# Splitting one more store of a DMA-bound rotary-score kernel over its DMA engines

## The chip, the cores and the metric

The kernel runs on one core of one Trainium2 chip. The metric is device time in microseconds (us), lower is better. A core has 16 DMA engines; "landing" means the semaphore update by which one of them reports that its part of a transfer has arrived.

## The reference

```python
batch, seq, heads, dim = 16, 512, 16, 64        # all float32
q_rot = concat([q1*cos - q2*sin, q1*sin + q2*cos])   # k_rot likewise
scores = einsum('bshd,bthd->bsht', q_rot, k_rot)     # (16, 512, 16, 512)
```

Inputs are 2 x 33.5 MB, the output is 268 MB. Writing it is most of the work.

## The kernel before

There are 64 steps, four per batch. A step makes 128 rows of one batch's output for all 16 heads in a staging tile of 128 x 8192 floats (4096 KB), copied there from PSUM by ACT, and stores it (the four steps of the first batch store theirs in parts of 1024 KB). There are three staging buffers.

```python
stage_pool = ctx.enter_context(tc.tile_pool(name="stage", bufs=3))
...
    def store(i, st):
        o = o_v[i // C, i % C]
        if i < NST - 1:                              # NST = 64, the number of steps
            nc.sync.dma_start(o, st)                 # 128 rows of 32 KB
            return

        h = H - 2
        nc.sync.dma_start(o[:, :h], st[:, :h])       # 14 heads, 128 rows of 28 KB
        nc.sync.dma_start(o[:116, h:], st[:116, h:]) # 2 heads, 116 rows of 4 KB
        nc.sync.dma_start(o[116:, h:], st[116:, h:]) # 2 heads, 12 rows
...
        nc.scalar.copy(out=so, in_=si)               # L173: PSUM to staging, 8 per step
```

128 rows are shared by 16 engines, 8 rows each. 116 = 4 x 29 rows go to the first four engines, 12 rows to twelve; the trace shows 16, 4 and 12 landings, and the prediction below says why. So a split store takes bytes off the other engines and gives them to the first four.

## Time and profile before

| | before |
|---|---|
| time, the first three runs | 800.7 us (800.0 to 800.71) |
| bytes moved, mean rate | 336.17 MB, 421 GB/s |
| DMA queue 1 busy | 98.6% of 16 engines' span |
| PE, ACT, DVE busy | 87%, 70%, 68% |

When a queue is busy 98.6% of the span on average, the average no longer tells much. What counts is the engine that ends last. The profile's views sum over the engines; the landings, read one by one from the trace, show the single engine. The prediction below shows both.

### The profile page before, as it was taken

How to read it: one execution, taken by the hardware profiler on the slowest of the kernel's cores; microseconds unless marked ns; L12 is line 12 of the kernel's file. 1: busy time of each engine (PE TensorE's matmuls, PEld its weight loads, DVE VectorE, ACT ScalarE, POOL GpSimd, SP SyncE). 2: the span in 40 equal slices, each digit the busy share in tenths (PEclk: the TensorE clock that was granted, in tenths of full speed). 3: DMA queues.
4: the chain of work that ended last, by engine and by line, in shares of the span. 5: the costliest groups of instructions: out<-in, count | busy, mean ns of one | idle time of the engine just before them, and what ended most of it. 6: DMA issues, size and time to landing. Idle time of an engine off the chain costs nothing.

```text
span 799.0 us, 7715 instructions
## 1 busy us (share of the span) xinstructions
PE 691.3 (87%) x3072; PEld 299.3 (37%) x3072; DVE 544.6 (68%) x516; ACT 561.2 (70%) x647; POOL 0.7 (0%) x6
## 2 busy tenths in 40 slices
PE   4989998997979979799797997979979799799970
PEld 2444443343434334343343443424434343344420
DVE  6999987676866768577585775857758478585300
ACT  3888886775857758577585775757757677578870
POOL 0000000000000000000000000000000000000000
PEclk9999999898998989889898898988989899899995
DMA  9999999999999999999999999999999999998995
GB/s 355 422 424 424 432 427 433 425 435 427 421 437 426 439 427 430 433 431 430 431 428 433 434 428 429 433 438 420 418 426 434 435 415 418 426 440 375 422 439 231
DMA packets 17844, 336.17 MB, mean 421 GB/s; under 512 B 1808, under 2 KB 3088, under 8 KB 4240
## 3 DMA queue, kind: packets, MB, share of 16 engines
q1 hardware_dynamic: 17520, 335.55, 98.6%
q8 instruction: 24, 0.39, 0.2%
q10 hardware_dynamic: 288, 0.13, 0.1%
q14 instruction: 12, 0.10, 0.0%
HBM read 67.24 MB, written 268.44 MB: 420 GB/s over the span
## 4 chain that ended last, share of the span: by engine, by line
DMA 50%; PE 40%; ACT 4%; DVE 3%; issue 1%; ACTq 0%; SPq 0%; DVEq 0%
DMA out_dram<-st 47%; PE ps L166 30%; PE bank L127 10%; ACT st L173 4%; DMA q_sb<-in_q_dram 2%; DVE part L106 1%; DMA early<-in_k_dram 1%; DVE q_sb L107 0%; DVE k_sb L107 0%; DVE k_sb L111 0%; DVE q_sb L111 0%; DVE early L107 0%; DVE kT_t L142 0%; ACTq L281 0%; DVE early L111 0%
## 5 line engine op out<-in xcount | busy, mean ns | idle before, releaser
L173 ACT COPY st<-ps 128x1024 f32<-128x1024 f32 x512 | 494.7, 1018 | 203.7 <-DMA out_dram<-st 105.6
L166 PE MATMUL ps<-kT_t,qT_t 64*128 64x512 f32 x2048 | 548.9, 654 | 71.0 <-ACT st L173 70.9
L166 PEld LDWEIGHTS ps<-kT_t,qT_t 64*128 64x128 f32 x2048 | 185.0, 197 | 261.7 <-issue 144.6
L142 DVE COPY qT_t<-bank 128x512 f32<-128x512 f32 x118 | 81.6, 691 | 203.8 <-PE bank L127 203.8
L127 PEld LDWEIGHTS bank<-ident,q_sb 128*128 128x128 f32 x480 | 55.6, 152 | 102.5 <-issue 99.1
L127 PE MATMUL bank<-ident,q_sb 128*128 128x128 f32 x480 | 86.9, 308 | 0.9 <-PE ps L166 0.9
L127 PEld LDWEIGHTS bank<-ident,k_sb 128*128 128x128 f32 x480 | 50.5, 141 | 95.4 <-issue 38.7
L127 PE MATMUL bank<-ident,k_sb 128*128 128x128 f32 x480 | 78.7, 287 | 1.6 <-DVE qT_t L142 1.2
L142 ACT COPY kT_t<-bank 128x512 f32<-128x512 f32 x122 | 72.5, 599 | 6.4 <-PE bank L127 6.4
L107 DVE TENSOR_TENSOR q_sb<-q_sb,cos_t 128x1024 f32<-128x1024 f32 x60 | 73.5, 1226 | 2.1
L111 DVE TENSOR_TENSOR k_sb<-k_sb,part 128x1024 f32<-128x1024 f32 x60 | 73.5, 1225 | 2.1
L107 DVE TENSOR_TENSOR k_sb<-k_sb,cos_t 128x1024 f32<-128x1024 f32 x60 | 73.5, 1225 | 2.0
L106 DVE TENSOR_TENSOR part<-q_sb,ss_t 128x1024 f32<-128x1024 f32 x60 | 73.5, 1225 | 2.0
L106 DVE TENSOR_TENSOR part<-k_sb,ss_t 128x1024 f32<-128x1024 f32 x60 | 73.0, 1216 | 0.1
L111 DVE TENSOR_TENSOR q_sb<-q_sb,part 128x1024 f32<-128x1024 f32 x60 | 73.0, 1216 | 0.0
L127 PE MATMUL bank<-ident,early 128*128 128x128 f32 x64 | 10.5, 316 | 12.5 <-DVE early L111 10.6
L127 PEld LDWEIGHTS bank<-ident,early 128*128 128x128 f32 x64 | 8.3, 161 | 17.5 <-issue 13.4
L106 DVE TENSOR_TENSOR part<-early,ss_t 128x1024 f32<-128x1024 f32 x8 | 9.8, 1223 | 5.9 <-DMA early<-in_k_dram 5.8
L111 DVE TENSOR_TENSOR early<-early,part 128x512 f32<-128x512 f32 x16 | 10.3, 687 | 0.2
L107 DVE TENSOR_TENSOR early<-early,cos_t 128x1024 f32<-128x1024 f32 x8 | 9.8, 1225 | 0.3
L142 ACT COPY qT_t<-bank 128x512 f32<-128x512 f32 x10 | 5.7, 617 | 3.2 <-PE bank L127 3.2
L142 DVE COPY kT_t<-bank 128x512 f32<-128x512 f32 x6 | 4.1, 685 | 0.3 <-PE bank L127 0.3
(9 smaller groups left out, 2.8 us busy)
## 6 DMA issues: line engine op xcount, KB each, us to landing
out_dram<-st SPq DMA_DIRECT2D x59, 4096.0 KB, 23.9
k_sb<-in_k_dram SPq DMA_DIRECT2D x15, 2048.0 KB, 26.9
q_sb<-in_q_dram SPq DMA_DIRECT2D x15, 2048.0 KB, 29.9
out_dram<-st SPq DMA_DIRECT2D x16, 1024.0 KB, 14.3
out_dram<-st SPq DMA_DIRECT2D x1, 3584.0 KB, 20.4
early<-in_k_dram SPq DMA_DIRECT2D x1, 1536.0 KB, 8.9
early<-in_q_dram SPq DMA_DIRECT2D x1, 1536.0 KB, 12.1
early<-in_k_dram SPq DMA_DIRECT2D x1, 512.0 KB
```

Of the source, the lines that this page charges most:

```text
L106: nc.vector.tensor_tensor(pv, xs, ss, op=mult)
L107: nc.vector.tensor_tensor(xc, xc, cs, op=mult)
L111: nc.vector.tensor_tensor(y, y, z, op=add)
L127: nc.tensor.transpose(bank[:, x, :], src, ident)
L142: copy(out=dst, in_=src)
L166: nc.tensor.matmul(out=po, lhsT=lhs[64 * r : 64 * r + 64, :], rhs=rh, start=True, stop=True)
L173: nc.scalar.copy(out=so, in_=si)
```

## The change

The intent is to take the split that the last store has and use it a second time, at step 56, so that the engine that ends last has less to write.

```diff
-        if i < NST - 1:
+        if i not in (NST - 8, NST - 1):
             nc.sync.dma_start(o, st)
             return
```

One transfer becomes three.

## The prediction

> **What bounds the kernel now.** I read the page from its DMA part first, because 336 MB pass in 799 us. These are the lines for queues and issues.
>
> ```profile
> DMA packets 17844, 336.17 MB, mean 421 GB/s; under 512 B 1808, under 2 KB 3088, under 8 KB 4240
> ...
> q1 hardware_dynamic: 17520, 335.55, 98.6%
> q8 instruction: 24, 0.39, 0.2%
> ...
> out_dram<-st SPq DMA_DIRECT2D x59, 4096.0 KB, 23.9
> ...
> out_dram<-st SPq DMA_DIRECT2D x1, 3584.0 KB, 20.4
> ...
> out_dram<-st SPq DMA_DIRECT2D x1, 464.0 KB
> ...
> out_dram<-st SPq DMA_DIRECT2D x1, 48.0 KB
> ```
>
> Queue 1 alone keeps the 16 DMA engines busy 98.6% of the span. PE is busy 87%, ACT 70%, DVE 68%. So the transfers bound the kernel, and the question is which of the 16 engines ends last. Next the busy time by stretches at the end (start:end, length, busy us of PE, PEld, DVE, ACT, POOL, granted clock, DMA share, GB/s).
>
> ```profile
> 700.00:727.00 27.00, 24.68 (x112) 10.43 (x108) 20.34 (x20) 19.65 (x24) 0.00 (x0) 0.94 1.00 431
> 727.00:731.00 4.00, 4.00 (x22) 1.72 (x19) 3.22 (x3) 3.77 (x6) 0.00 (x0) 1.00 0.35 147
> 731.00:789.00 58.00, 42.91 (x192) 18.01 (x190) 13.64 (x15) 38.12 (x42) 0.00 (x0) 0.91 1.00 426
> 789.00:795.00 6.00, 0.00 (x0) 0.00 (x0) 0.00 (x0) 0.00 (x0) 0.00 (x0) 0.50 0.30 107
> 795.00:799.00 4.00, 0.00 (x0) 0.00 (x0) 0.00 (x0) 0.00 (x0) 0.00 (x0) 0.50 0.04 15
> ```
>
> Two holes: from 727 to 731 the engines are two thirds idle, and after 789 only a few work; a share of 0.04 is less than one engine of 16 (0.0625). The views do not name an engine, so I read the trace's packet and semaphore records one by one. Every store ends in 16 landings, one per engine. In us, by step, with the time of issue:
>
> ```
> step issued  earliest ... latest but one   last
> 55   695.98  708.02       712.80           719.46
> 56   706.00  717.70       722.48           729.33
> 57   716.02  727.38       732.18           739.30
> 58   730.22  741.14       743.23           749.88
> 60   748.85  760.92       762.57           769.72
> 62   767.60  780.38       782.41           789.24
> 63   777.43  788.89       790.87           797.80  (14 heads)
> 63   778.35  794.22 to 794.95 (4 landings: 116 rows, 2 heads)
> 63   779.10  12 landings, 11 by 795.13, the last 797.99
> ```
>
> **One engine, the straggler, is always last**, 9 to 12 us behind the fastest. Its packets follow each other without a gap from 731 to 797.6 (back-to-back records). It takes about 9.9 us per full store, the others 9.68. The end is its end.
>
> The chain of waits says the same: it goes through store 60 into ACT's first copy of step 63 (start, length, what).
>
> ```profile
> 748.85 20.87 DMA out_dram<-st
> ...
> 769.82 1.02 ACT st L173
> ...
> 777.40 0.92 ACTq L281
> ```
>
> The staging pool has three buffers, so step 63 starts only when all 16 engines have delivered store 60, which is the straggler's 769.72. Steps 62 and 58 do likewise (ACT's timeline):
>
> ```profile
> 719.56 3.84 ACT L173 COPY st<-ps 128x1024 f32<-128x1024 f32 x4 [3.56 <-DMA out_dram<-st]
> ...
> 759.92 7.65 ACT L173 COPY st<-ps 128x1024 f32<-128x1024 f32 x8 [2.30 <-DMA out_dram<-st]
> ```
>
> The line at 719.56 makes the hole: step 58 waits for store 55's last landing (719.46), its store is issued only at 730.22, and by then fast engines have been out of work since 727.4.
>
> **What the Trainium skill says.** "DMA: Bandwidth & Descriptors", section "Why a DMA increments its semaphore by 16 and not by 1": the number of engines is the largest k up to 16 that divides the slowest dimension, on the lowest-numbered engines. So 116 rows go to 4 engines (29 rows each), 12 rows to 12, 128 to 16. The trace agrees: 4 and 12 landings above. The straggler is among the 12, since 797.99 belongs to the 12-row transfer, and not among the first four, which land by 794.95. Same page, "Specifications": about 27 GiB/s an engine; the trace has 32,768 B in 1.213 us, 27.0 GB/s, so the engine is at its rate. Same page, "Latency and other measured facts": engines 7 and 15 are usually slower, put down there to the descriptor rings of GpSimd's path. The trace has one slow engine although GpSimd issues nothing, so the reason given does not fit; the records do not number engines, so whether it is 7 is open.
>
> **The change, part by part.** It takes one 4096 KB store away and puts 3584 KB, 464 KB and 48 KB in its place. Bytes and all compute are the same.
>
> On the straggler: 8 packets of 32,768 B (8 x 1.213 = 9.70 us) become 8 of 28,672 B (1.062 us each in the last store, 8.50) plus one of 4,096 B (0.159) and two more semaphore packets (0.009 each): 8.67. It saves **1.03 us**. It has no gap afterwards, so this should reach the end whole: its last packet at 796.6 instead of 797.63.
>
> On engines 0 to 3: 8 x 1.062, then 29 and 1 packets of 4,096 B. In the last store these 30 took about 5.3 to 6.1 us (the shortest, 0.159 each, would make 4.8). Sum 13.3 to 14.6 against 9.70: **3.6 to 4.9 us more** on each. The hole pays for it if they are among the engines that wait in it. Following packets back to back through the trace, I find 7 engines at 727.4 to 728.0 after step 57, 8 at 728.7 to 732.2, and the straggler. The 8 are those that take turns at the instruction packets of queue 8 (24 packets, three each, some 0.9 us each). Two of those 8 that fetch at 736.6 and 766.1 are single-row engines (4 to 11) in the last store; one engine of the first four fetches from queue 14 at 754.8, and no queue-8 fetch is seen on it. The best reading, not a proof, is that engines 0 to 3 are all in the fast seven. Their last packets of step 57 end at 727.0 to 727.6 (a landing is recorded some 0.36 us after its packet), so they now end at 730.6 to 732.5, while step 58's packets start at 731.05 to 731.20 anyway: a slip of 0 to 1.5 us, with 0.3 us more room at 741. Their last landing goes from 794.95 to between 794.9 and 796.2, still ahead of the straggler's 796.8.
>
> Other parts: two more issues on SP (0.70 and 1.19 us in the last store). SP idles about 10 us between stores and step 57's store comes at 716.02, so they are hidden. Step 59 on ACT now waits for three semaphores instead of one, an estimate of 0.1 us; but store 56 should be complete by 728.3, before step 59 starts at 731. Steps 61 to 63 start up to 1 us earlier, which matters only to the already queued work.
>
> Sum: -1.03 us on the path that sets the end. 800.7 - 1.0 = **799.7 us**, that is 0.13%.
>
> **The rivals.** (1) Engines 0 to 3 take over as the bound. If one is among the lagging eight (730.5 or later), it leaves step 57 at 734 to 737, 3 to 6 us late, and ends at 798 to 800: gain gone or a loss of up to 2 us, 800 to 802.5. For it: the identity is inferred. Against: the fetch pattern. One in six. (2) The gain is eaten before the end: the straggler gets more instruction packets (one of 8 KB cost it 0.34 us at 745.0), or slow 4 KB packets (some took 0.3 to 0.76 us right after 788.6). Then 800.0 to 800.6. (3) The earlier landing at step 56 shifts the start of later steps and closes more of the waiting: 799 or a little below. Against: the straggler has no gap to close, it is simply its bytes.
>
> **Range and chances.** Three runs of before spread 0.71 us by themselves (800.0 to 800.71), nearly the size of the effect. Main reading 799.3 to 800.0; with that spread and rival 1 or 2, 798.9 to 800.7. No rival makes 2% (16 us): faster 0.01, same 0.98, slower 0.01.
>
> **What would show it.** The issue table with 4096 KB x58 and 464 KB x2; the last landing of step 56 at about 728.3 and, of its part on four engines, 721 to 722.5; less idle DMA between 727 and 731 (share above 0.35); ACT's waits that ended at 759.92 and 769.82 ending about 1 us earlier; the last landing near 796.8 with the four engines before it. The prediction is wrong if the four engines land last, if the straggler is not about 1 us earlier from step 56 on, or if step 58's store is issued at another time than 730.2.

## The result

The changed kernel took 800.53 us (median of 6 runs, 799.92 to 801.33), the kernel before 800.38 us (6 runs, 800.0 to 800.71). The ratio is 1.0003, with an interval of 0.999 to 1.0015: the same. The 1.0 us that was predicted (a ratio of 0.9987) is not to be seen in it, and lies just outside its interval.

The profiled run was the slowest of the six (801.33 us). Its page, the issues that changed:

```profile
out_dram<-st SPq DMA_DIRECT2D x58, 4096.0 KB, 24.0
...
out_dram<-st SPq DMA_DIRECT2D x2, 3584.0 KB, 23.9
...
out_dram<-st SPq DMA_DIRECT2D x2, 464.0 KB
```

The split is there twice, as intended. Busy time by stretches of the same run (columns as in the prediction):

```profile
727.00:731.00 4.00, 4.00 (x22) 1.85 (x22) 3.87 (x4) 3.77 (x6) 0.00 (x0) 1.00 0.71 303
731.00:789.00 58.00, 42.71 (x200) 17.87 (x196) 14.86 (x16) 39.55 (x43) 0.00 (x0) 0.92 0.98 419
789.00:795.00 6.00, 0.00 (x0) 0.00 (x0) 0.00 (x0) 0.00 (x0) 0.00 (x0) 0.50 0.55 203
795.00:799.50 4.50, 0.00 (x0) 0.00 (x0) 0.00 (x0) 0.00 (x0) 0.00 (x0) 0.50 0.08 31
```

The hole after 727 has shrunk from a share of 0.35 to 0.71, and after 789 more engines work. Such windows mislead here, though, because this run as a whole is shifted. The chain of waits shows by how much:

```profile
697.38 23.67 DMA out_dram<-st
...
721.15 1.02 ACT st L173
...
750.44 19.85 DMA out_dram<-st
...
770.38 6.51 ACT st L173 x7
...
776.89 0.92 ACTq L281
```

Store 55 is complete at 721.05 us (697.38 + 23.67). In the kernel before it was complete at 719.46, as its own chain shows:

```profile
695.98 23.48 DMA out_dram<-st
...
719.56 1.02 ACT st L173
```

The instructions up to there are the same in both kernels, so the run was 1.59 us late before it reached the change. ACT's timeline gives the two later waits:

```profile
760.46 7.65 ACT L173 COPY st<-ps 128x1024 f32<-128x1024 f32 x8 [1.60 <-DMA out_dram<-st]
770.38 7.43 ACT L173 COPY st<-ps 128x1024 f32<-128x1024 f32 x8 [2.28 <-DMA out_dram<-st]
```

In the kernel before, the first of them ended at 759.92 (the line is in the prediction), the second here:

```profile
769.82 4.74 ACT L173 COPY st<-ps 128x1024 f32<-128x1024 f32 x5 [2.25 <-DMA out_dram<-st]
```

As absolute times they are 0.54 and 0.56 us later than before. Counted from store 55's completion they are 39.41 and 49.33 us, where the kernel before has 40.46 and 50.36. They came 1.05 and 1.03 us earlier. So I measured everything that follows **from the last landing of step 55 to the last landing of all**, and call it the tail. It leaves out what happens before the change. The landings, read from the trace:

```
                          before    changed
step 55, last landing     719.46    721.05
step 56, last, 14 heads   729.33*   729.70      (*all 16 heads)
step 56, last, all parts  729.33    729.90
step 63, four engines     794.95    796.32      (116 rows)
step 63, last of all      797.99    798.46
tail                       78.53     77.40      -1.13 us
```

At step 56 itself the straggler needed 9.87 us before (729.33 - 719.46) and 8.85 us now (729.90 - 721.05), 1.02 us less. The other 0.1 us of the 1.13 came in the steps after it; no run says why.

### The profile page after: what moved, and what is told of

The parts are those of the page before. It is cut to its first block, busy times and chain, and to the rows that moved or that the text cites. A ratio compares the mean times of both kernels' runs of the same rounds, so it can differ in the third digit from the quotient of the medians.

```text
span 799.5 us, 7719 instructions
## 1 busy us (share of the span) xinstructions
PE 688.9 (86%) x3072; PEld 299.3 (37%) x3072; DVE 544.5 (68%) x516; ACT 561.4 (70%) x647; POOL 0.7 (0%) x6
## 4 chain that ended last, share of the span: by engine, by line
DMA 48%; PE 38%; DVE 5%; ACT 5%; issue 1%; ACTq 0%; DVEq 0%
DMA out_dram<-st 48%; PE ps L166 28%; PE bank L127 9%; ACT st L173 5%; DVE part L106 2%; DVE early L111 1%; DVE k_sb L111 1%; DVE k_sb L107 1%; DVE early L107 1%; DMA early<-in_k_dram 1%; DVE kT_t L142 0%; DVE q_sb L107 0%; DVE q_sb L111 0%; ACTq L281 0%; DVE qT_t L142 0%
```

## The experiments

Twelve kernels ran, in four groups; each group shares a chip and has its own runs of the kernel before. First the table, then what each was for. Times are medians with the range of the runs; the tail comes from the one profile of each.

| label | what differs | tail, us | step 55 complete | time, us | ratio to before (interval) |
|---|---|---|---|---|---|
| (before) | last store split | 78.53 | 719.46 | 800.38 | 1 |
| (changed) | 56 and 63 split | 77.40 | 721.05 | 800.53 (799.92 to 801.33) | 1.0003 (0.999 to 1.0015) |
| null | as before | 78.51 | 719.78 | 800.95 (800.31 to 804.99) | 1.0003 (0.9984 to 1.0022) |
| after_again | as changed | 77.39 | 719.67 | 800.1 (799.45 to 802.82) | 0.9993 (0.9976 to 1.0011) |
| after_third | as changed | 77.40 | 719.13 | 799.54 (798.91 to 800.71) | 0.9986 (0.9975 to 0.9998) |
| no_split | no store split | 79.47 | 719.76 | 801.38 (801.04 to 801.98) | 1.0002 (0.9989 to 1.0015) |
| only56 | 56 alone | 78.39 | 718.95 | 801.2 (800.13 to 802.44) | 0.9997 (0.9984 to 1.001) |
| at60 | 60 in place of 56 | 80.11 | 720.64 | 804.33 (802.38 to 807.18) | 1.0041 (1.0021 to 1.006) |
| seven_56 | 119 rows, 7 engines | 85.02 | 719.73 | 806.3 (805.71 to 807.65) | 1.0062 (1.0048 to 1.0075) |
| six_56 | 114 rows, 6 engines | 84.27 | 718.38 | 806.05 (805.53 to 808.64) | 1.0076 (1.0063 to 1.0088) |
| five_56 | 125 rows, 5 engines | 86.51 | 719.36 | 808.5 (807.84 to 808.89) | 1.0095 (1.0082 to 1.0108) |
| wide_56 | 119 rows, 4 heads | 90.27 | 719.04 | 811.3 (808.76 to 812.19) | 1.012 (1.0101 to 1.0138) |
| five_heads | 56 alone, 124 rows, 5 heads | 86.22 | 718.85 | 808.53 (804.35 to 812.88) | 1.0099 (1.0072 to 1.0125) |
| four_heads | 56 alone, 124 rows, 4 heads | 81.84 | 720.28 | 803.42 (802.93 to 806.29) | 1.0039 (1.0022 to 1.0056) |

The expectations give 78.3 and 77.2 us for the tails of the kernel before and the changed one where the table has 78.53 and 77.40. They counted to the landing of the 14 heads; the table counts to the last landing of any part.

### What can be resolved: null, after_again, no_split, at60

`null` is the kernel before with a comment changed.

> The kernel before with one comment changed. Every theory: ratio 1.000; its interval and its spread (800.0 to 800.7 so far) measure what the comparison can resolve. If the 1.6 us by which the profile after was late already at step 55 is plain scatter, this kernel's landings of step 55's last engine differ from 719.46 by as much (0.5 to 2 us) from profile to profile.

The tail is 78.51 us, 0.02 from that of the kernel before. Store 55 is complete at 719.78, only 0.32 us from 719.46: less than the 0.5 to 2 us that the expectation gave for plain scatter, so this run alone does not explain 721.05. The whole time is the same, but its interval is 0.9984 to 1.0022: plus or minus 1.5 us. This comparison cannot resolve 1 us, while the tail can.

`after_again` is the changed kernel with a comment changed.

> The changed kernel with one comment changed. Theory BYTES (the split takes 1.0 to 1.1 us off the straggler and the end is the straggler's): ratio 0.9987 (about -1.0 us), and from step 55's last landing to the end's last landing 77.2 us against 78.3 in the kernel before. Rival OFFSET (the changed program is 1 us later before step 56 for a lasting reason, such as two more DMAs in the program): ratio 1.000 to 1.001, step 55's last landing again near 721 while the null kernel has 719.5. Rival NOTHING (the end is set by something else): 78.3 us from step 55 to the end.

The tail is 77.39 us, within 0.01 of the first profile, and store 55 is complete at 719.67, not 721. So OFFSET, a lasting delay ahead of step 56, falls. NOTHING falls too. The time came out 0.07% lower, in the same wide interval.

`no_split` takes both splits away:

```diff
-        if i not in (NST - 8, NST - 1):
+        if i not in ():
```

> No store is split, not even the last. BYTES: the straggler carries one row-part more, ratio to before 1.0013 (+1.0 us), from step 55's last landing to the end 79.3 to 79.4 us; all engines but the straggler end near 790. NOTHING: ratio 1.000 and 78.3 us.

The tail is 79.47 us. One split is thus worth 79.47 - 78.53 = 0.94 us at the end and the second 78.53 - 77.40 = 1.13 us: BYTES is right in the tail. The straggler alone is left at the end, as this row of the stretches shows (0.05 is less than one engine of 16):

```profile
795.00:800.00 5.00, 0.00 (x0) 0.00 (x0) 0.00 (x0) 0.00 (x0) 0.00 (x0) 0.50 0.05 20
```

The time shows nothing clear (1.0002), so the split that the kernel before already had can't be seen in the whole time either.

`at60` moves the second split behind the idle stretch:

```diff
-        if i not in (NST - 8, NST - 1):
+        if i not in (NST - 4, NST - 1):
```

> The split is moved from step 56, before the idle stretch of the fast engines (727 to 731), to step 60, after it. Theory HOLE (the idle stretch pays for the four engines): the straggler ends 1 us earlier than before, but the first four engines carry 4.4 us more with no idle stretch to pay, land at about 799.3 instead of 794.95 and set the end: ratio 1.0018 (+1.5 us). Rival BYTES ALONE (place does not matter): ratio 0.9987, four engines still before the straggler.

It is clearly slower, 1.0041 (3.3 us, where HOLE expected 1.5), and its tail is 1.58 us longer than that of the kernel before. The 116 rows of the last store land at 798.61 to 800.58, against 794.22 to 794.95, and set the end, as HOLE expected: counted from store 55's completion the last of them lands at 79.94 us against 75.49, 4.45 us later (expected: 4.4). The straggler, however, is not 1 us earlier, as HOLE also expected: its 14 heads land 78.75 us after store 55, against 78.34 before. What made the whole time longer than the tail does is not shown. The place of the split matters: at step 56 the four engines pay from time that they would have idled. The chain of waits of this run also starts from a small part of the split store, the 12 rows issued at 749.20:

```profile
748.45 0.69 SPq L152
749.14 0.06 issue
749.20 20.73 DMA out_dram<-st
...
770.03 6.51 ACT st L173 x7
```

One thing came unforeseen. While the four engines wrote their 4 KB packets (759 to 766 us), at least twenty packets of 32 KB, which began between 759.7 and 765.3, took 1.34 to 2.07 us instead of 1.213, and near the end one 28 KB packet of the straggler took 2.507 us instead of 1.062. In `no_split`, by contrast, only seven large packets after 700 us took over 1.33 us, none over 1.82. In the changed kernel's first profile, six 32 KB packets starting between 718.7 and 721.4 took 1.44 to 1.87 us, and one 28 KB packet at 792.3 took 2.414; there it was not the straggler's. Between 716 and 722 us, `after_again` and `only56`, which split step 56 too, have seven 32 KB packets above 1.33 us each; `after_third` has none, though it splits the same store, and neither have the kernel before, `null` and `no_split`. So slow packets come where the split is, but not each time. That the size of the small packets makes them, and not the uneven load on four engines, is not shown.

### Is the scatter made by the small packets? only56

```diff
-        if i not in (NST - 8, NST - 1):
+        if i != NST - 8:
```

> Only step 56 is split, the last store is whole: the change alone, without the older split at the end. BYTES: straggler 1.1 us earlier than with no split, from step 55's last landing to the end 78.3 to 78.4 us (79.47 with no split, 78.53 in the kernel before). Theory STALL (packets of 4 KB on four engines slow the large packets of other engines, and at the end nothing is left to absorb a stall, so runs with the last store split scatter): the runs of this kernel lie close together as those without split did (spread about 1 us, 801.0 to 802.0), and no run is 3 us above its median; ratio 0.999 to 1.000. Rival CHIP NOISE: outliers of 3 to 4 us here as in the kernel before.

The tail is 78.39 us, 1.08 us under `no_split`, as BYTES says. The scatter is inconclusive: 2.3 us between the runs (800.13 to 802.44), more than `no_split` has (0.9 us), but with no outlier of 3 us; and the runs of the kernel before in this group had none either (800.05 to 802.22). So whether the small packets make the scatter stays open.

### Which engine is the straggler? seven_56, five_56, six_56, wide_56

The four kernels change the number of rows, and with it the number of engines that share them (`wide_56` also has `h = H - 4`).

```diff
-        nc.sync.dma_start(o[:116, h:], st[:116, h:])
-        nc.sync.dma_start(o[116:, h:], st[116:, h:])
+        nc.sync.dma_start(o[:119, h:], st[:119, h:])   # 125 in five_56, 114 in six_56
+        nc.sync.dma_start(o[119:, h:], st[119:, h:])
```

> Both split stores leave 119 rows instead of 116 to the transfer of their own, so 7 engines share it (17 rows each) and 9 rows go to 9 engines. If the straggler is not among the first seven engines: it again loses 7 row-parts, 77.4 us from step 55's last landing to the end, and the engines that take the rows carry about 2.1 us more instead of 4.4, so they end near 791.5, far before the straggler; STALL then expects a smaller scatter and ratio 0.9987. If the straggler is one of the first seven, it carries 2 us more per split store: 81 to 82 us and ratio 1.004.

> As the one with 119 rows, but the last four heads instead of two (rows of 8 KB). BYTES: the straggler loses twice as much in each of the two stores, 2.1 us each, so from step 55's last landing to the end 79.47 - 4.2 = 75.2 us; the seven engines carry about 3.2 us more each, of which the idle stretch pays the first, and end near 792. Ratio 0.996 (-3.2 us against the kernel before). If another engine takes over (one that fetches instructions, or the seven): above 76.5 us.

Both are clearly slower (tails of 85.02 and 90.27 us), so the straggler is one of the seven; the sizes were missed (81 to 82 us were expected for this outcome in `seven_56`, and 75.2 in `wide_56` if no other engine took over). With 116 rows it is not one of the four. The landings of the last store's 119 rows show it: six engines at 794.95 to 796.39, one at 804.57. In ACT's timeline the wait for step 59's buffer, which ended with the straggler's part of store 56, is new:

```profile
732.25 2.84 ACT L173 COPY st<-ps 128x1024 f32<-128x1024 f32 x3 [3.36 <-DMA out_dram<-st]
```

> 125 rows on five engines (25 each), 3 rows on three, in both split stores. The run with 119 rows put the straggler among engines 4 to 6. If it is 5 or 6: it loses all 8 row-parts of 4 KB, 8 x 0.151 = 1.2 us per split store, so from step 55's last landing to the end 79.47 - 2.4 = 77.1 us (77.4 with 116 rows), the five carry about 3.4 us more; ratio 0.9985. If it is 4: it carries about 3.4 us more twice, 85 us or more, ratio 1.008.

> 114 rows on six engines (19 each), 14 rows on fourteen. If the straggler is engine 6: 77.4 us from step 55's last landing to the end, the six carry about 2.5 us more instead of 4.4 and end near 792; ratio 0.9987 with little scatter. If it is 4 or 5: it carries 2 to 3 us more twice, near 84 us, ratio 1.006. With the run of 125 rows this names the engine.

With 125 rows on five engines the straggler is still among them: 5 landings, four at 795.15 to 795.58 and one at 805.88. Six engines tell the same (802.47 against 794.20 at most). By the Trainium skill's rule that a transfer takes the lowest-numbered engines ("DMA: Bandwidth & Descriptors", "Why a DMA increments its semaphore by 16 and not by 1"), the sets are nested; four leave it out and five do not: it is the **fifth engine**. The decisive pair, 116 rows in `after_third` (below) and 125 rows here, ran on the same chip. Why this engine is slow, no run tells. That is why 116, a multiple of four, is a good number of rows here and 119, 114 and 125 are bad ones.

### Pooling: after_third

The changed kernel once more, in one group with the last two.

> The changed kernel a third time, to pool. SCATTER (what comes before step 55 varies by 0.5 to 2 us from run to run, for every kernel, and hides the gain): 77.4 us from step 55's last landing to the end again, step 55's last landing anywhere from 719 to 721, ratio between 0.998 and 1.000. OFFSET (changed program lastingly later before step 56): step 55 at 720.5 or later, ratio 1.000 or more.

The tail is 77.40 us, as in both others, and store 55 is complete at 719.13. OFFSET falls for the second time. The ratio is 0.9986, with an interval of 0.9975 to 0.9998. The three comparisons of the same two kernels thus gave 1.0003, 0.9993 and 0.9986 against an expected 0.9987. Weighted by their intervals, they make 0.9994, plus or minus 0.0008 (an estimate from the three intervals): 0.5 us faster, give or take 0.6. That excludes neither no gain nor the predicted 1.0 us. In whole times the gain is not shown.

The margin is small, though: in this profile the four engines' last landing of 116 rows is at 796.27 us, the straggler's 14 heads land at 796.34, and the end is at 796.53. So the four ended 0.26 us ahead of the end; in the kernel before it was 3.04 us (797.99 - 794.95), in the other two profiles of the changed kernel 2.14 us and 1.12 us. The stretches of this run cannot show this: in the mean six engines of 16 work between 789 and 795 (a share of 0.36), and less than one after that.

```profile
789.00:795.00 6.00, 0.00 (x0) 0.00 (x0) 0.00 (x0) 0.00 (x0) 0.00 (x0) 0.50 0.36 134
795.00:798.00 3.00, 0.00 (x0) 0.00 (x0) 0.00 (x0) 0.00 (x0) 0.00 (x0) 0.50 0.04 18
```

### A better version? five_heads, four_heads

The runs pointed to one larger split at step 56, on four engines, with the last store whole. Both kernels were misses.

```diff
-        if i not in (NST - 8, NST - 1):
+        if i != NST - 8:
...
-        h = H - 2
+        h = H - 5                                   # H - 4 in four_heads
-        nc.sync.dma_start(o[:116, h:], st[:116, h:])
-        nc.sync.dma_start(o[116:, h:], st[116:, h:])
+        nc.sync.dma_start(o[:124, h:], st[:124, h:])
+        nc.sync.dma_start(o[124:, h:], st[124:, h:])
```

> A candidate that the runs so far point to: the straggler is the fifth engine, so four is the widest transfer that leaves it out; one split only, at step 56, with five heads (rows of 10 KB) of 124 rows on the first four engines (31 each) and 4 rows on the same four, and the last store whole, so that no small packets run at the end. BYTES: the straggler loses 8 x 5 x 2 KB = 81,920 B, 3.0 us, so from step 55's last landing to the end 79.47 - 3.0 = 76.4 us; the four engines carry about 9.1 us more, the idle stretch pays some 3.7, they end near 794.3. Ratio 0.9975 (-2.0 us against the kernel before, -1 against the changed one). If the four engines or stalls set the end: 77.5 us or more and ratio 0.999 or above.

> The same with four heads (rows of 8 KB), a smaller load on the four engines. BYTES: the straggler loses 65,536 B, 2.4 us: 77.0 us from step 55's last landing to the end, the four engines carry 7.5 us more and end near 793. Ratio 0.998 (-1.5 us). If it comes out faster than the one with five heads, the four engines or the stalls, not the straggler, limit that one.

The bytes left the straggler as planned, but the four engines took its place. Their 10 KB packets took 598 ns in the mean where the shortest took 385, and the 8 KB packets 499 ns against 309; the medians are 393 and 309 ns, so a part of the packets were slowed a great deal. The 124 rows of five heads landed only at 730.93 to 736.87 us. Step 59 had to wait for that buffer:

```profile
737.39 2.84 ACT L173 COPY st<-ps 128x1024 f32<-128x1024 f32 x3 [7.81 <-DMA out_dram<-st]
```

The wait of 7.81 us delayed the store of step 59 to 749.44, which idled the other engines. My estimate used the shortest packet time for wide rows, and that was its mistake. Why packets of 8 and 10 KB take over half as long again in the mean on four engines beside full stores, where the 4 KB packets of step 56 in the changed kernel had a mean of 173 ns with both kinds of part counted and a shortest of 159, no run settles. No version here is known to beat both kernels.

## Why the prediction was right or wrong

- **Time and range.** Predicted 799.7 us within 798.9 to 800.7, and the same with 0.98; measured 800.53 us. The range held, and the verdict too, but neither tests the mechanism: both would have held with no gain at all, as the kernel before was 800.38 us in the same rounds. A gain of 1.0 us was predicted; the first comparison shows none, and all three together 0.5 us, give or take 0.6.
- **The bound is one straggler.** Right: it was last in every landing list of the kernel before and in the three profiles of the changed one. With both splits away it ends alone. It is not always alone in lagging: in two profiles of the changed kernel the latest landing but one of store 55 came at 719.22 us (straggler 721.05) and 717.91 (719.13), where the kernel before has 712.80 (719.46). This was before the change, so another engine is sometimes slow too.
- **Its saving, 1.03 us, "should reach the end whole".** Right in the tail: 1.11 to 1.14 us in three profiles of the changed kernel against two of the one before. Against `no_split`, `only56` shows 1.08 us. At step 56 alone it is 1.01 to 1.04 us (8.83 to 8.85 us in the three, 9.86 and 9.87 in the two), so the sum of packet times was right, and rival 2, which eats the gain before the end, did not come. One slip: the last landing forecast near 796.8 should read 797.0 (797.99 - 1.03); 796.8 fits the 14 heads. Also, the 27.0 GB/s of the trace are 25.2 GiB/s, 7% less than the 27 GiB/s that the prediction sets beside them.
- **The hole pays for the first four engines.** Right, shown by `at60`. Their 116 rows of step 56 landed at 722.57 to 723.88 us in the first profile; the prediction's 721 to 722.5 shifted by that run's 1.59 us is 722.6 to 724.1. In `after_again` and `after_third` the last of them came at 723.78 and 724.50, 1.1 and 2.3 us after the range shifted in the same way. Counted from store 55's completion, their last landing of 116 rows came at 75.27, 76.28 and 77.14 us in the three profiles, against 75.49 before (`null`: 76.16); the slip predicted was 0 to 1.5 us. Measured against 75.49 it was -0.22, 0.79 and 1.65 us, so once it was larger. That the four are all among the fast seven was inferred, and no run names them. In `after_third` they came within 0.1 us of the straggler's 14 heads, so rival 1 is close though it did not win in a profile.
- **What was under-rated.** The prediction took the spread of three runs, 0.71 us, for the noise. The completion of store 55, in profiles of kernels whose instructions are the same up to there, ranges from 718.38 to 721.05 us, 2.7 us or more than twice the effect. That is where the predicted gain went in the first comparison's profile: that run was 1.59 us late before the change and 1.13 us faster after it, and its last landing is 0.47 us later than before. That the mean of the six runs has the same cause is likely but not shown, as only one trace per kernel is kept.
- **What was missed.** While four engines write their 4 KB packets, large packets of other engines can be slow. In the three profiles of the changed kernel it did not touch the straggler's tail; in `at60` it did, with a packet 1.45 us longer (2.507 - 1.062). How often it does in unprofiled runs is open.
- **Rival 3**, closing the wait further, got no support: from store 55's completion to step 58's issue it is 10.76 us before and 10.75 us after. As an absolute time step 58's store was issued at 731.80 and not at 730.2, which the prediction had named as a sign of being wrong; the 1.59 us by which the run was late before the change make this difference.

## What to carry to other kernels

When a queue is near 100% busy, list the landings of each transfer by engine: the end can be that of one slow engine, and the number of rows decides which engines share a transfer. Before moving bytes from the slow engine to others, look for a stretch in which those others idle anyway, and put the extra work just ahead of it. When an effect is smaller than the scatter of whole runs, measure it from a common event just ahead of the change; a tail that repeats to 0.02 us shows 1.1 us that six whole runs did not. Such a tail says that the mechanism works; it does not say that the whole kernel is faster, and here that stayed open.

## What the Trainium skill lacked or had wrong

- "DMA: Bandwidth & Descriptors", "Latency and other measured facts": it names engines 7 and 15 as usually slower, with GpSimd's descriptor rings as a best guess at the cause. Here the slow engine is the fifth of the lowest-numbered ones (116 rows on four engines leave it out: tail 77.40 us; 125 rows on five take it in: 86.51 us), and no transfer was issued from GpSimd. The records do not number engines, so whether 7 and 15 lag behind the rest cannot be seen. The slow one took about 9.9 us per 4096 KB store, the others 9.68.
- "DMA: Bandwidth & Descriptors", "Why a DMA increments its semaphore by 16 and not by 1": the rule of the divisor held for 116, 119, 114, 125, 124 and 12 rows (4, 7, 6, 5, 4 and 12 landings). What it lacks is the cost of a divisor that takes in a slow engine: with two split stores the tails were 7 to 9 us longer (84.27 to 86.51 against 77.40).
- No page that I read tells that large packets can be slow while a few engines write small ones: 1.34 to 2.07 us instead of 1.213 for at least twenty packets in `at60`. Nor that packets of 8 and 10 KB on four engines then take 499 and 598 ns in the mean against a shortest of 309 and 385.
- No page that I read tells how instruction packets are spread: the 24 packets of queue 8 (16 KB each) took 0.88 to 0.97 us each in the kernel before, and the fifth and sixth of every eight took 0.88 to 0.89 where the others took 0.93 to 0.97. This fits eight engines that take turns, three packets each, as also found by following packets back to back; it is not a proof.
